# The tenth pair of feature tiles by seven products, with the squares of x summed beside the pairs

## The chip, the cores and the metric

The kernel runs on one core of a Trainium2 chip. The metric is the device time of one execution in microseconds (us). The core has TensorE (PE in the profile, with its weight loads as PEld), VectorE (DVE), ScalarE (ACT), GpSimd (POOL) and SyncE (SP); SP and POOL issue nearly all transfers (DMAs).

## The reference

A trunk of two layers over 512 tokens of width 1024. Layer 0 has latent attention, layer 1 has chunked attention over a shared key and value band; both then have the feed-forward part that the change is in, with a norm ahead of it and one behind it:

```python
def rms_norm(x, g):
    xf = x.astype(jnp.float32)
    y = xf * lax.rsqrt(jnp.mean(xf * xf, axis=-1, keepdims=True) + EPS)
    return (y * g.astype(jnp.float32)).astype(x.dtype)

def swiglu(h, w_gate, w_up, w_down):
    return (jax.nn.silu(h @ w_gate) * (h @ w_up)) @ w_down

for layer in range(DEPTH):
    ...
    x = x + rms_norm(y, attn_post_g[layer])
    h = rms_norm(x, ffn_pre_g[layer])
    f = swiglu(h, ffn_w_gate[layer], ffn_w_up[layer], ffn_w_down[layer])
    x = x + rms_norm(f, ffn_post_g[layer])
```

The feed-forward width is 2816, which is 22 tiles of 128 features.

## The kernel before

Every product of two matrices is computed as three matmuls: each operand is split into a high part (a cast, on ScalarE) and a low part (the remainder, subtracted on VectorE), and high by high, high by low and low by high are added up. `split` (L143 to L145) does this for a chunk of weights of 128 x 1024. The high parts and the low parts of weights have three buffers each, taken in turn, so the fourth chunk's cast waits until the first has been read.

`ffn` runs for each layer. It begins with the output projection of the attention (`out_proj`), in two halves of 256 tokens. Behind each half `Post.apply` norms the result and adds the residual x (L672, L674), which `fetch` has loaded (L683), and splits the new x, times the gain of the next norm, into `xh` and `xl` (L148, L149). The norm's row factor is left out there and comes in later, as a row `rb` that is multiplied into the gate's result.

The 22 tiles of gate and up weights are then treated in three ways:

- tiles 0 and 1 by halves of the tokens, `half(h)`, so that the first can start before the second half of x is there;
- tiles 2 and 3 by whole products, 512 tokens wide, `proj(2, KT, 4, ...)` (L377 to L379): 4 outputs (gate and up of two tiles) x 8 blocks of depth x 3 = 96 matmuls;
- the other 18 tiles as nine pairs in `products`: a product of two-by-two blocks by seven products instead of eight (the scheme of Strassen and Winograd, here on token halves, depth halves and the two tiles of a pair). Each of the seven products, numbered j = 0 to 6, is 24 matmuls of 256 columns (L1550); it needs one chunk of weights (a quarter of the weights or a sum of quarters) and one block or sum of blocks of x.

The outputs of the seven products go to banks of the accumulator memory named be (j = 0 and 6), al (j = 1, 3, 4, 5) and ga (j = 2). `gate` and `up_` (gt and ut) gather them: copies by ScalarE (L1554, L1556, L1560, L1564) and additions by VectorE (L1558, L1562, L1566). Behind j = 6 the pair is finished: gt is multiplied by rb (L1567), ScalarE takes its silu, VectorE multiplies by ut into a hidden tile hd (L1570), and `Hidden` makes sums of hidden tiles (hs, L1271 to L1274) for the down projection, which uses the same seven products.

The sums of weights for a pair: two are formed by DMAs that accumulate into a loaded tile, issued by POOL (L171), two by VectorE (L184). For the first pair, whose `begin` nothing calls, VectorE forms all of them. The sums of x (the `th` and `tl` tiles, made in steps by `blocks_of`) stand beside the whole products.

The squares of the new x are made by ScalarE and added up by VectorE in `sx.squares` (L459, L463) half by half. `total` transposes the sum on TensorE (`tot`, L473) and reduces it; `rstd` takes the power on POOL (L483); `spread_sb` puts the row across partitions by four transposes on TensorE (`bc`, L501) and a copy. Both sets of transposes stand among the whole products. The new x is stored to `mid` in memory ahead of the whole products; the layer's last norm loads it again.

In which order each engine runs its instructions is set when the program is built: a scheduler places them by priorities (`first`, `some`, `weave`, the place in the code) and by explicit orders (`issue_after`); each engine then runs its list in order and waits where an operand or a buffer isn't ready.

Of the kernel before, what the change touches and what calls it, by code (L numbers as in the profile page):

```python
# [19 lines left out]
KT = D // P  # L20
# [7 lines left out]
N_WHOLE = 4  # L28
# [40 lines left out]
def trunk(ctx: ExitStack, tc: tile.TileContext, a, out):  # L69
# [73 lines left out]
    def split(dst_hi, dst_lo, src):  # L143
        return (nc.scalar.copy(dst_hi, src),  # L144
                V.tensor_tensor(dst_lo, src, dst_hi.bitcast(F32), op=OP.subtract))  # L145

    def split_scaled(dst_hi, dst_lo, src, col):
        return (nc.scalar.activation(dst_hi, src, AF.Copy, scale=col),  # L148
                V.scalar_tensor_tensor(dst_lo, src, col, dst_hi.bitcast(F32), op0=OP.mult, op1=OP.subtract))  # L149

    class Pair:
# [4 lines left out]
        def __init__(self, src):  # L156
            self.src, self.raw, self.then, self.made = src, {}, None, False

        def tile(self, n, pool_=wp, tag="raw", bufs=5):
            t = pool_.tile([P, 1024], F32, tag=tag, name=name_("raw"), bufs=bufs)  # L160
            nc.sync.dma_start(t, self.src[n])
            return t

        def begin(self):

            r, self.made = self.raw, True
            r[0] = r[3] = r[6] = self.tile(2, wide[0], "sum", 2)
            r[4] = self.tile(2, wide[0], "sum2", 2)
            for j, n in ((0, 3), (4, 0)):
                with tc.issue_after(last_pow[0].ins):  # L170
                    nc.gpsimd.dma_start(r[j], self.src[n], accum_op=OP.add)  # L171

        def load(self, j):

            if j == 0:
                if not self.made:
                    self.raw[4] = self.tile(2, wide[0], "sum2", 2)
                self.raw[5] = self.tile(3)
            elif j in (1, 2):
                self.raw[j] = self.tile(j - 1)  # L180

        def sums(self, j):
# [4 lines left out]
            if j == 0 and not self.made:  # L187
                r[0] = r[3] = r[6] = wide[0].tile([P, 1024], F32, tag="sum", name=name_("raw"), bufs=2)
                plus(r[0], r[4], r[5])
            elif j in (3, 6):  # L190
                plus(r[j], r[j], r[j // 3])
            elif j == 4 and not self.made:
                plus(r[4], r[4], r[1])
            elif j == 1 and self.then:
# [69 lines left out]
    class Feed:  # L264


        def __init__(self):
            self.plan, self.raw, self.ready, self.pos, self.room = [], [], [], 0, {}
            self.behind, self.gate, self.low = {}, None, None
# [4 lines left out]
        def add_pairs(self, src):  # L274
# [3 lines left out]
            for p, pair in enumerate(pairs):  # L278
                pair.then = pairs[p + 1] if p + 1 < n else None
                for j in range(7):  # L280
                    self.plan.append((pair, 1024, j, None))
# [7 lines left out]
        def load(self, i):  # L289
            while len(self.raw) <= min(i, len(self.plan) - 1):  # L290
# [5 lines left out]
                if isinstance(src, Pair):  # L296
                    src.load(j)
# [8 lines left out]
        def split(self, i):  # L306
            while len(self.ready) <= min(i, len(self.plan) - 1):
# [32 lines left out]
                for c in range(0, 0 if isinstance(raw, list) else n, w):  # L340
                    m = min(w, n - c)
                    with ExitStack() as st:
                        for b in self.behind.get(j, ()):
                            st.enter_context(tc.issue_after(b.ins))
                        if gain is None or isinstance(src, Pair):
                            self.low = split(pieces[c // w][0][:, :m], pieces[c // w][1][:, :m], raw[:, c:c + m])[1]
# [92 lines left out]
    class Sum:  # L439
# [28 lines left out]
        def total(self, h=None, ahead=0):  # L468
# [3 lines left out]
            for i in q:  # L472
                nc.tensor.transpose(t[:, i * P:(i + 1) * P], self.acc[:, i * P:(i + 1) * P], ident)  # L473
# [22 lines left out]

    def spread(col, first=0):

        b = bank("t", "bc")
        for i in range(col.shape[1]):  # L500
            nc.tensor.transpose(b[:, (first + i) * P:(first + i + 1) * P],  # L501
                                col[:, i:i + 1].to_broadcast([P, P]), ident)
# [109 lines left out]
    class Post:  # L612
# [21 lines left out]
        def add_half(self, h, banks, rest, n1, n2, end=None):  # L634
# [7 lines left out]
            with first(200):  # L642
                r = rstd(v)
                fence = V.tensor_copy(small("f")[:, :v.shape[1]], r),
            for n in range(len(feed.ready), len(feed.ready) + 6):
# [21 lines left out]
        def apply(self, x, h, each, to=None):  # L667
            c = HALF[h]
            for k in range(KT):
                t = self.y[k][:, c]  # L670
                with first(80 * h):
# [5 lines left out]
                    each(k, h)  # L677

    def fetch(src, make=U):
        x = []  # L680
        for k in range(KT):
            t = make(name="x")
            nc.sync.dma_start(t, src[:, k])  # L683
            x.append(t)
        return x

    def out_proj(rhs, n_k, post, have, n_last, late):
# [35 lines left out]
        for h in range(2):  # L723
# [17 lines left out]
            if not h:  # L741
                feed.ahead(2 if late else 3)
        return b
# [39 lines left out]
    def plan_ffn(i):  # L783
        for c in range(4):
            feed.add(a["w_gu0"][i, c], 1024, room="h")
        for f in range(N_WHOLE - 2):
            for c in range(2):
                feed.add(a["w_gu"][i, f, c], 1024)
# [345 lines left out]
    def ffn(i, x_src, osp, firsts, late=()):  # L1134
# [10 lines left out]
        x = fetch(x_src)  # L1145
        post = Post(G_APOST[i], H)
        last = out_proj(osp, KT, post, firsts, 2, late)
# [17 lines left out]
        post.add_half(1, last, rest, 9, 14)  # L1165
        run(rest)
        sx.squares(0)
        post.apply(x, 1, sx.each)
        run(half(1))
        sx.squares(1)  # L1170
        for k in range(KT):
            nc.sync.dma_start(a["mid"][:, k], x[k])
        tb = []
        more = blocks_of(x, G_FPRE[i], H, tb)
        next(more)
# [6 lines left out]
        V.tensor_scalar(eps, v, EPS, None, op0=OP.mult)  # L1182
        some(rest, 7)
        rb = spread_sb(r)
        next(more)
        banks.extend(b)
        hid = Hidden(H)


        for f in range(N_WHOLE):  # L1190
            if f < 3:
                b = banks[2 * f:2 * f + 2]
                if f == 2:
                    run(rest)
            else:
                b = [bank(), bank()]
                run(proj(2, KT, 4, xs, b))
            t = U(name="gt")
            V.tensor_tensor(t, b[0], rb, op=OP.mult)
            nc.scalar.activation(t, t, AF.Silu)  # L1200
            h = hid.room()
            V.scalar_tensor_tensor(h, t, -1.0, b[1], op0=OP.mult, op1=OP.mult)
            hid.add(h)
            if f == 1:
                next(more)
        products(xs, tb, rb, hid, by_tokens(H) if i else None)
# [108 lines left out]
    def blocks_of(x, gain, make, out):  # L1315
# [3 lines left out]
        for k in range(KT // 2):  # L1319
# [538 lines left out]
```

## Time and profile before

| | |
|---|---|
| median of 3 runs | 1106.17 us (1105.13 to 1106.2) |
| the profiled execution | 1105.07 us, of which 1103.3 are its span |
| granted TensorE clock, mean of the span | 0.997 of full speed |
| memory read / written in the span | 148.88 MB / 10.88 MB |
| matmuls | 6893 |

The page's rows on engines give busy time, share of the span and number of instructions. A row of the chain in order of time gives start, length, engine, tile and line; a row of a group gives the line, engine, operation and tiles, then how often, busy us and mean ns of one, and the idle time of the engine just before them with its releaser. A row of the DMA issues gives the queue (SPq, POOLq), the count, the size and the median us from issue to landing. Line numbers in the profile are those of the kernel before.

### The profile page before, as it was taken

The page shows a single profiled execution, that of the slowest core. Times are in us where ns is not written, and L with a number is a line of the kernel's source. Part 1 is how long each engine was busy: PE and PEld are TensorE (multiplying, and loading weights), DVE is VectorE, ACT ScalarE, POOL GpSimd, SP SyncE. Part 2 cuts the span into 40 slices and gives each one's busy share as a digit, 9 for nine tenths or more (in the row PEclk, how much of TensorE's full clock was granted, in tenths as well). Part 3 has the DMA queues.
Part 4 walks back from the last instruction along what each step waited for, and adds up shares of the span by engine and source line. Part 5 has one row for each costly group of instructions (what it writes and reads, how often), then busy time and mean ns, then how long its engine had stood idle before and what let it go on. Part 6 is the DMA issues. An engine that isn't in the chain of part 4 may idle for free.

```text
span 1103.3 us, 19079 instructions
## 1 busy us (share of the span) xinstructions
PE 1092.4 (99%) x6893; PEld 978.8 (89%) x6893; DVE 908.5 (82%) x1659; ACT 678.3 (61%) x1323; POOL 117.1 (11%) x181
## 2 busy tenths in 40 slices
PE   9999999999999999999999999999999999999997
PEld 6887889999999998888888888889899999998885
DVE  7787747988878889978858898758988889789977
ACT  7575737655555556668636767657645555556675
POOL 2211100101000001500000110000100010001401
PEclk9999999999999999999999999999999999999999
DMA  7344226447787757961555677634638888758913
GB/s 240 120 116 142 62 68 238 143 116 184 171 202 184 180 167 248 164 191 49 190 153 156 173 192 186 168 121 161 198 103 214 228 207 223 216 178 249 171 29 76
DMA packets 88334, 181.47 MB, mean 164 GB/s; under 512 B 26816, under 2 KB 28608, under 8 KB 88240
## 3 DMA queue, kind: packets, MB, share of 16 engines
q1 hardware_dynamic: 74752, 147.10, 43.1%
q0 software_dynamic: 13056, 32.73, 16.4%
q8 instruction: 54, 0.88, 0.3%
q10 hardware_dynamic: 432, 0.44, 0.1%
q14 instruction: 40, 0.33, 0.1%
HBM read 148.88 MB, written 10.88 MB: 145 GB/s over the span
## 4 chain that ended last, share of the span: by engine, by line
PE 97%; DVE 1%; ACT 1%; issue 1%; DMA 0%; POOL 0%; DVEq 0%; POOLq 0%; SPq 0%; ACTq 0%
PE al L1550 19%; PE b L377 11%; PE b L378 11%; PE b L379 11%; PE be L1550 9%; PE al L1306 8%; PE be L1306 5%; PE ga L1550 5%; PE de L1306 3%; PE ga L1306 3%; PE pt L561 2%; PE b L1707 2%; PE b L1107 1%; PE sc L1699 1%; PE sc L1698 1%
## 5 line engine op out<-in xcount | busy, mean ns | idle before, releaser
L144 ACT CAST whi<-raw 128x1024 fp32r<-128x1024 f32 (+3 forms) x220 | 221.0, 1006 | 205.6 <-PE al L1550 71.5
L145 DVE TENSOR_TENSOR wlo<-raw,whi 128x1024 fp32r<-128x1024 f32 (+3 forms) x220 | 255.8, 1164 | 67.1 <-ACT whi L144 66.1
L1550 PE MATMUL al<-th,whi 128*128 128x256 f32 x432 | 122.8, 284 | 0.0
L1550 PE MATMUL al<-th,wlo 128*128 128x256 f32 x432 | 121.0, 280 | 0.0
L1550 PE MATMUL al<-tl,whi 128*128 128x256 f32 x432 | 121.0, 280 | 0.0
L377 PE MATMUL b<-xh,whi 128*128 128x512 f32 x234 | 96.7, 415 | 0.0
L378 PE MATMUL b<-xl,whi 128*128 128x512 f32 x234 | 91.8, 392 | 0.0
L379 PE MATMUL b<-xh,wlo 128*128 128x512 f32 x234 | 91.7, 392 | 0.0
L1550 PEld LDWEIGHTS al<-th,whi 128*128 128x128 f32 x432 | 81.3, 188 | 2.2
L1550 PEld LDWEIGHTS al<-th,wlo 128*128 128x128 f32 x432 | 81.3, 188 | 0.2 <-DVE wlo L145 0.2
L1550 PEld LDWEIGHTS al<-tl,whi 128*128 128x128 f32 x432 | 81.3, 188 | 0.0
L548 ACT ACTIVATE p<-p,mn 128x128 f32<-128x128 f32 (+1 forms) x96 | 54.1, 563 | 36.0 <-DVE mn L546 34.1
L145 DVE TENSOR_TENSOR ptl<-pt,pth 128x128 fp32r<-128x128 f32 (+1 forms) x96 | 46.6, 485 | 30.5 <-ACT pth L144 29.6
L145 DVE TENSOR_TENSOR wlo<-wd,whi 128x512 fp32r<-128x512 f32 x86 | 56.3, 684 | 14.6 <-ACT whi L144 14.4
L144 ACT CAST whi<-wd 128x512 fp32r<-128x512 f32 x86 | 49.8, 618 | 25.0 <-PE al L1306 10.7
L144 ACT CAST pth<-pt 128x128 fp32r<-128x128 f32 (+1 forms) x96 | 40.3, 422 | 32.2 <-PE pt L561 31.3
L171 POOL DMA_DIRECT2D raw<-in_w_pair x32 | 28.1, 895 | 285.9 <-DVE ut L1562 84.1
L379 PEld LDWEIGHTS b<-xh,wlo 128*128 128x128 f32 x234 | 43.9, 188 | 9.9 <-DVE wlo L145 0.3
L1306 PE MATMUL al<-whi,pl 128*128 128x512 f32 x132 | 51.5, 390 | 0.0
L1306 PE MATMUL al<-wlo,ph 128*128 128x512 f32 x132 | 51.4, 389 | 0.0
L1306 PE MATMUL al<-whi,ph 128*128 128x512 f32 x132 | 51.4, 389 | 0.0
L377 PEld LDWEIGHTS b<-xh,whi 128*128 128x128 f32 x234 | 44.2, 189 | 5.7 <-ACT whi L144 0.2
(320 smaller groups left out, 3391.2 us busy)
## 6 DMA issues: line engine op xcount, KB each, us to landing
raw<-in_w_pair SPq DMA_DIRECT2D x88, 512.0 KB, 4.6
raw<-in_w_pair POOLq DMA_DIRECT2D x32, 512.0 KB, 7.6
wd<-in_w_down SPq DMA_DIRECT2D x54, 256.0 KB, 6.0
raw<-in_w_o SPq DMA_DIRECT2D x16, 512.0 KB, 4.0
raw<-in_w_gu SPq DMA_DIRECT2D x16, 512.0 KB, 4.7
raw<-in_w_down SPq DMA_DIRECT2D x16, 512.0 KB, 4.3
raw<-in_w_qkb SPq DMA_DIRECT2D x16, 512.0 KB, 3.5
wd<-in_w_down POOLq DMA_DIRECT2D x22, 256.0 KB, 5.0
```

The source lines that it names most:

```text
L144: return (nc.scalar.copy(dst_hi, src), V.tensor_tensor(dst_lo, src, dst_hi.bitcast(F32), op=OP.subtract))
L145: V.tensor_tensor(dst_lo, src, dst_hi.bitcast(F32), op=OP.subtract))
L171: nc.gpsimd.dma_start(r[j], self.src[n], accum_op=OP.add)
L377: nc.tensor.matmul(o, l[0], r[0], start=start, stop=False)
L378: nc.tensor.matmul(o, l[0], r[1], start=False, stop=False)
L379: last_mm[0] = nc.tensor.matmul(o, l[1], r[0], start=False, stop=stop)
L548: nc.scalar.activation(p[:, :n], p[:, :n], AF.Exp, bias=mn[:, :1], scale=-1.0, accum_out=self.sums[:, qt:qt + 1])
L561: nc.tensor.transpose(t[:, kt * P:(kt + 1) * P], p[:, kt * P:(kt + 1) * P], ident)
L1107: nc.tensor.matmul(o[:, q_], va[kt][:, part, v_], pt[:, kt, q_], start=n + kt == 0, stop=n == 2 and kt == NQT - 1)
L1306: nc.tensor.matmul(to[e], l[c], r[d], start=j < 4 and k == 0 and n == 0, stop=k == NF // 2 - 1 and n == 2, skip_group_check=True)
L1550: nc.tensor.matmul(o, l[c], r[d], start=first_ and n == 0, stop=k == K2 - 1 and n == 2, skip_group_check=True)
L1707: nc.tensor.matmul(o[:, q_], vv, pt[:, kt, q_], start=pt is pth and kt == 0, stop=pt is ptl and kt == NQT - 1)
```

## The change

`N_WHOLE` goes from 4 to 2: tiles 2 and 3 are no longer computed by whole products but join the pairs, of which there are now ten, and the array of weights for the whole products goes. What stood beside the whole products is placed elsewhere:

- The first pair takes its products in the order 1, 2, 0, 3, 6, 4, 5. All its sums of weights are formed by accumulating DMAs, one into the next (`begin`, `chain`), begun in the half stage.
- x's fetch is ordered behind a load of weights further on (`get_x`), and its token sums are made in more steps, some in the half stage, some beside the first pair.
- x's squares are made beside the first pair: eight by ScalarE, four additions by VectorE, and three accumulating DMAs on POOL's queue (`squares`, `add_squares`). `norm` totals them in the second pair, with an explicit order: product 4 of the second pair stands behind the `tot` transposes, and the third pair's first product behind the `bc` transposes. The results of tiles 0 and 1 are copied out of the accumulator banks (`kept`, fu) until the row is there.
- Finishing a pair (times rb, silu, times ut, the hidden sums) is put into a list of `units`. One is let out at product 6 of the second pair, and from the third pair on one at each of products 1, 3 and 5.
- x is stored to `mid` in the third pair, a block at each product.
- In layer 1 the side work of `by_tokens` (loads, transposes and stores of x for the last norm) starts behind the fifth pair, eight steps a pair, instead of behind the first with four.

```diff
-N_WHOLE = 4
+N_WHOLE = 2
...
+    FIRST_TURN = (1, 2, 0, 3, 6, 4, 5)
...
+        def add(self, j, src, after=None):
+            with behind(after or last_pow[0]):
+                return nc.gpsimd.dma_start(self.raw[j], src, accum_op=OP.add)
+
+        def chain(self):
+
+            self.add(3, self.raw[0])
+            self.add(4, self.src[0], self.add(6, self.raw[3]))
...
             if not h:
                 feed.ahead(2 if late else 3)
+                feed.loaded = get_x(feed.loads[feed.pos + (4 if late else 5)])
...
-        for k in range(KT):
-            nc.sync.dma_start(a["mid"][:, k], x[k])
...
-        b = [bank(), bank()]
-        rest = proj(2, KT, 4, xs, b)
-        some(rest, 3)
-        v = sx.sum.total()
-        r = rstd(v)
...
+        def squares(ks):
+            for k in ks:
+                sq.append(H(name="sq"))
+                nc.scalar.activation(sq[k], x[k], AF.Square, scale=D ** -0.5)
+
+        def add_squares():
+            n = KT // 2
+            for k in range(n):
+                V.tensor_tensor(sq[k], sq[k], sq[k + n], op=OP.add)
+            for n in (2, 1):
+                for k in range(n):
+                    last_pow[0] = nc.gpsimd.dma_start(sq[k], sq[k + n], accum_op=OP.add)
...
+        def norm():
+            sx.sum.acc = sq[0]
+            v = sx.sum.total(None, 300)
+            at[1, 4] = sx.sum.last
...
+        def spread_():
+            rb[0] = spread_sb(rb[0])
+            at[2, 0] = last_bc[0]
...
+        side = {(0, 2): step, (0, 3): step_, (0, 5): add_squares, (1, 3): norm, (1, 6): spread_}
+        side.update(((2, j), lambda j=j: store(j)) for j in range(7))
+        side[3, 0] = lambda: store(7)
+        units = [lambda f=f: gate(*kept[2 * f:2 * f + 2]) for f in range(N_WHOLE)]
+        products(xs, tb, rb, hid, side, units, empty, at, by_tokens(H) if i else None)
...
-            for j in range(7):
-                if aside is not None and p and j in (0, 1, 3, 5):
+            for j in (range(7) if p else FIRST_TURN):
+                if (p, j) in side:
+                    side[p, j]()
+                if p and j in ((6,) if p == 1 else (1, 3, 5)) and units:
+                    units.pop(0)()
+                for _ in range(1 + (j == 3) if aside is not None and p > 4 else 0):
                     next(aside, None)
                 w = feed.next(1024, 2)
+                done = at.get((p, j)) if p else mm
...
                     else:
                         V.tensor_tensor(t[:, A1], t[:, A1], o, op=OP.add)
-                        V.tensor_tensor(t, t, rb, op=OP.mult)
-                        nc.scalar.activation(t, t, AF.Silu)
-                        h = hid.room()
-                        V.tensor_tensor(h, t, u, op=OP.mult)
-                        hid.add(h)
+                        units.append(lambda t=t, u=u: gated(t, u))
+                        while p > 6 and units:
+                            units.pop(0)()
```

Two places in the order of the built program. First TensorE in the second pair (p = 1) of layer 0 of the change. The numbers behind names are buffer numbers; whi and wlo are the high and low parts of a chunk of weights, 2964 and 2965 those of product 3, 3074 and 3075 those of product 6.

```order
L1635 MATMUL al_2969<-tl_2492,whi_2964 128x256
L1635 MATMUL al_2969<-th_2491,wlo_2965 128x256
L1635 MATMUL be_2925<-xh_2286,whi_3074 128x256
L1635 MATMUL be_2925<-xl_2287,whi_3074 128x256
L1635 MATMUL be_2926<-xh_2286,whi_3074 128x256
L1635 MATMUL be_2926<-xl_2287,whi_3074 128x256
L1635 MATMUL be_2925<-xh_2286,wlo_3075 128x256
L1635 MATMUL be_2925<-xh_2292,whi_3074 128x256
```

The last two matmuls of product 3 are followed by product 6, first the four that need only its high part. Sixteen rows on, the same list goes over to the transposes of the squares' sum and to product 4 (weights 2998 and 2999):

```order
L1635 MATMUL be_2926<-xh_2292,wlo_3075 128x256
L1635 MATMUL be_2926<-xh_2298,whi_3074 128x256
L489 MATMUL tot_3030<-ident,sq_2712 128x128 x4
L1635 MATMUL al_2968<-th_2481,whi_2998 128x256
```

So 19 of the 24 matmuls of product 6 stand ahead of `tot` and of products 4 and 5; the other five stand behind the `bc` transposes, at the end of the pair. In the program of before the pairs' products stand in their numbers' order; here the end of a second pair and the first matmuls of a third:

```order
L1550 MATMUL be_2859<-xh_2293,whi_3007 128x256
L1550 MATMUL be_2859<-xl_2294,whi_3007 128x256
L1550 MATMUL be_2859<-xh_2293,wlo_3008 128x256
L1550 MATMUL be_3119<-th_2606,whi_3037 128x256
L1550 MATMUL be_3119<-tl_2607,whi_3037 128x256
```

Second, VectorE at the beginning of the third pair (p = 2) of layer 0. Before, the finishing of the second pair stands among the third pair's subtractions:

```order
L145 TENSOR_TENSOR wlo_3074<-raw_2939,whi_3073 128x1024
L1566 TENSOR_TENSOR gt_2860<-gt_2860,be_2858 128x256
L1567 TENSOR_TENSOR gt_2860<-gt_2860,bc_2714 128x512
L1566 TENSOR_TENSOR gt_2861<-gt_2861,be_2859 128x256
L1567 TENSOR_TENSOR gt_2861<-gt_2861,bc_2714 128x512
L145 TENSOR_TENSOR wlo_3126<-raw_2974,whi_3125 128x1024
L1570 TENSOR_TENSOR hd_3092<-gt_2860,ut_2862 128x512
L1570 TENSOR_TENSOR hd_3109<-gt_2861,ut_2863 128x512
```

In the change the units of tiles 0 and 1 (fu) and of the first pair (gt_2666) stand there:

```order
L146 TENSOR_TENSOR wlo_3152<-raw_2996,whi_3151 128x1024
L1241 TENSOR_TENSOR fu_2639<-fu_2639,bc_3139 128x512
L1656 TENSOR_TENSOR gt_2928<-gt_2928,be_2926 128x256
L146 TENSOR_TENSOR wlo_3189<-raw_3041,whi_3188 128x1024
L1241 TENSOR_TENSOR fu_2641<-fu_2641,bc_3139 128x512
L1244 SCALAR_TENSOR_TENSOR hd_3143<-fu_2639,fu_2640 128x512
L1598 TENSOR_TENSOR gt_2666<-gt_2666,bc_3139 128x512
L146 TENSOR_TENSOR wlo_3235<-raw_2889,whi_3234 128x1024
L1244 SCALAR_TENSOR_TENSOR hd_3221<-fu_2641,fu_2642 128x512
```

From wlo_3152 to the addition that product 5 of the third pair waits for (ut_3185, L1652) the list has 24 instructions in the change: seven 1024 wide, eight 512 wide, nine 256 wide; before, the same stretch (wlo_3074 to ut_3123, L1562) has 20: seven 1024 wide, four 512 wide and nine 256 wide.

More of the change, by code (lines that the diff above doesn't have):

```diff
@@ L676, in apply, with fetch, out_proj @@
                         (nc.gpsimd if k in (0, 2, 4) else V).tensor_tensor(to(k), x[k][:, c], t, op=self.op)
[L677 to L687 removed]
+                    at = each(k, h)
+            return at
+    def fetch(src, x, after=None):
+        with behind(after):
+            for k in range(KT):
+                t = U(name="x")
+                ins = nc.sync.dma_start(t, src[:, k])
+                x.append(t)
+        return ins
+    def out_proj(rhs, n_k, post, have, n_last, late, get_x):
         done = list(have)
@@ L1177, in ffn @@
-        rest = proj(2, KT, 4, xs, b)
-        some(rest, 3)
-        v = sx.sum.total()
-        r = rstd(v)
-        eps = sp.tile([P, 4], F32, tag="eps", name=f"eps_{i}", bufs=1)
[L1182 to L1199, printed above, removed]
+        base = feed.pos
@@ new lines, in ffn @@
+        pair = feed.plan[base][0]
+        pair.chain()
+        feed.behind[base + 2] = feed.behind[base + 3] = post.apply(x, 1, sx.each)
+        next(more)
+        feed.ahead(3)
+        run(half(1))
+        kept = [H(name="fu") for _ in banks]
+        for t, b in zip(kept[:2], banks[:2]):
+            nc.scalar.copy(t, b)
+        with behind(next(more)[0]):
+            for t, b in zip(kept[2:], banks[2:]):
+                empty = nc.scalar.copy(t, b)
+        eps = sp.tile([P, 4], F32, tag="eps", name=f"eps_{i}", bufs=1)
```

172 lines of the change are left out of this document (108 added, 64 removed).

## The prediction

> **What bounds the kernel now.** I read the page's busy times first, then its chain of work that ended last, then that chain in order of time around the place that changes, then a table of stretches, and last the timelines of VectorE and ScalarE inside one pair.
>
> ```profile
> PE 1092.4 (99%) x6893; PEld 978.8 (89%) x6893; DVE 908.5 (82%) x1659; ACT 678.3 (61%) x1323; POOL 117.1 (11%) x181
> PE 97%; DVE 1%; ACT 1%; issue 1%; DMA 0%; POOL 0%; DVEq 0%; POOLq 0%; SPq 0%; ACTq 0%
> ```
>
> TensorE is busy for 99% of the span, and 97% of the chain is its own work. A matmul taken away is therefore worth its own time, and a wait put in front of TensorE costs its own length: there is no slack in which it could vanish. VectorE, at 82%, is the engine with the least to spare behind it.
>
> ```profile
> 212.23 0.23 PE b L377
> ...
> 214.30 0.44 PE tot L473 x4
> ...
> 219.55 0.44 PE bc L501 x4
> ...
> 234.75 0.23 PE b L379
> 234.98 2.82 PE be L1550 x24
> 237.80 2.82 PE al L1550 x24
> 240.61 2.81 PE ga L1550 x24
> ```
>
> This is the chain in layer 0: start, length, what ran. The 96 whole products of feature tiles 2 and 3 run from 212.23 to 234.98 us, with the four transposes of the squares (0.44) and the four that spread the row norm (0.44) among them; then the first pair starts, 24 matmuls in 2.82 us for each of its seven products. TensorE never pauses.
>
> ```profile
> 212.23:234.98 22.75, 22.75 (x106) 18.80 (x106) 20.60 (x42) 13.89 (x24) 2.90 (x3) 1.00 0.39 92
> 787.36:810.08 22.72, 22.72 (x107) 18.80 (x106) 20.09 (x43) 13.78 (x24) 3.22 (x3) 1.00 0.31 70
> 234.98:254.89 19.91, 19.91 (x170) 19.78 (x170) 16.56 (x24) 10.93 (x18) 0.86 (x1) 1.00 0.58 159
> 810.08:830.00 19.92, 19.92 (x170) 19.76 (x169) 17.68 (x25) 11.01 (x17) 0.83 (x1) 1.00 0.50 152
> ```
>
> The columns are the stretch, its length, and the busy time of PE, PEld, DVE, ACT and POOL, then the granted clock, the DMA share and GB/s. Rows one and two are the whole products of the two layers, rows three and four the first pair of each. The clock is 1.00 in all. VectorE is filled to 20.60 of 22.75 us in the stretch that goes, and to 16.56 of 19.91 in a pair.
>
> **The change part by part.**
>
> *The products.* In each layer 96 matmuls of 512 columns go and one pair of 168 matmuls of 256 columns comes. The eight transposes remain. Layer 0: 22.75 - 0.88 = 21.87 us go, 19.91 come: 1.96 us less. Layer 1: 22.72 - 0.88 - 19.92 = 1.92 less. Together **-3.88 us**. By the count of columns alone one eighth of 21.87, 2.73 us a layer, would go; the difference is what the smaller matmuls cost (19.91 / 168 = 0.1185 us for 256 columns, 21.87 / 96 = 0.2278 for 512, so 0.1139 for 256). The Trainium skill says, in Perfetto Trace Analysis, section Optimizing Tensor Performance, that larger matmuls are more efficient than smaller ones; this trace agrees, by 4%, and that is already in the sum above.
>
> *The place of pair 1's last product.* The order excerpt shows that TensorE now runs 19 matmuls of product 6 of pair 1 (weights whi_3074, wlo_3075) straight behind product 3, ahead of the transposes of the squares' sum and of products 4 and 5. There are three buffers for the high parts of weights, so product 6 takes the buffer of product 3, and its cast can start only when product 3 has read it. In the profile of before a pair's seven casts go through the same buffers, but for the order on TensorE; here are some of the second pair's:
>
> ```profile
> 263.26 1.05 ACT L144 CAST whi<-raw 128x1024 fp32r<-128x1024 f32 x1 [1.45 <-PE ga L1550]
> 266.12 1.05 ACT L144 CAST whi<-raw 128x1024 fp32r<-128x1024 f32 x1 [0.96 <-PE al L1550]
> 267.20 1.22 DVE L145 TENSOR_TENSOR wlo<-raw,whi 128x1024 fp32r<-128x1024 f32 x1 [1.63 <-ACT whi L144]
> 269.08 1.05 ACT L144 CAST whi<-raw 128x1024 fp32r<-128x1024 f32 x1 [1.65 <-PE al L1550]
> ```
>
> These are ScalarE's casts and one of VectorE's subtractions (start, length, what, and the idle time before it with what ended that). That pair starts at 254.89, so its product 3 ends four times 2.82 later, at 266.17: the cast of 266.12 is product 6's, released by product 3, done at 267.17; the low part follows from 267.20 to 268.42. So product 6's weights are there 1.0 us (high) and 2.25 us (low) after product 3's end. Before the change, products 4 and 5 (5.64 us) lay over this. Now TensorE stands there: it can do four matmuls that need only the high part (0.47 us), and waits for the rest: 2.25 - 0.47 = **1.8 us**. Behind these matmuls in TensorE's queue stand the transposes and products 4 and 5, whose weights are ready but which can't pass. The transposes also wait for VectorE's addition behind product 6's first half, covered by the five matmuls of the second half (0.59 us against one 256-wide addition): 0 to 0.2.
>
> *Units that were finished in the whole part or in their own pair and now come late.* The gate, silu and Strassen sums of tiles 0 and 1 and of pairs 0 and 1 can't run until the row norm is spread, which now happens behind pair 1. They are let out from the end of pair 1 on, and the order excerpt of VectorE shows them among pair 2's weight subtractions. From wlo_3152 (freed by product 5 of pair 1) to the addition that product 5 of pair 2 waits for, VectorE has 24 instructions: seven of 1024 columns, eight of 512, nine of 256. Their spacing, from a busy stretch of before:
>
> ```profile
> 259.01 1.22 DVE L145 TENSOR_TENSOR wlo<-raw,whi 128x1024 fp32r<-128x1024 f32 x1
> 260.14 0.42 DVE L1272 SCALAR_TENSOR_TENSOR hs<-hs,hd 128x256 f32<-128x256 f32 x1
> 260.48 0.42 DVE L1273 TENSOR_TENSOR hs<-hd,hd 128x256 f32<-128x256 f32 x1
> 260.81 0.42 DVE L1274 SCALAR_TENSOR_TENSOR hs<-hs,hd 128x256 f32<-128x256 f32 x1
> 261.15 1.22 DVE L184 TENSOR_TENSOR raw<-raw,raw 128x1024 f32<-128x1024 f32 x1
> 262.28 1.22 DVE L145 TENSOR_TENSOR wlo<-raw,whi 128x1024 fp32r<-128x1024 f32 x1
> ...
> 274.57 0.69 DVE L1567 TENSOR_TENSOR gt<-gt,bc 128x512 f32<-128x512 f32 x1
> 275.18 0.41 DVE L1566 TENSOR_TENSOR gt<-gt,be 128x256 f32<-128x256 f32 x1
> ```
>
> Start to start: 1.14 (259.01 to 260.14, 261.15 to 262.28), 0.335 and 0.61. So 7 x 1.14 + 8 x 0.60 + 9 x 0.335 = 15.8 us, starting one cast and a hand-over (1.05 + 0.2) behind the end of pair 1's product 5: done 17.05 us behind it. TensorE gets there after the transposes (0.44), five matmuls left of product 6 (0.59), five products (14.1) and three matmuls (0.35): 15.5 us. It waits **1.6 us**. This term is the difference of two long sums: if VectorE is 5% quicker it is 0.8, if one of its instructions waits for ScalarE's table load or silu it is 2.5. Bounds 0 to 2.5. Pair 3 has a unit more than it makes, too, and I add 0.2.
>
> *Pair 0.* Its sums of weights are now a chain of accumulating DMAs, begun in the half stage, so VectorE is spared two 1024-wide additions; in exchange VectorE gets the token sums that it had beside the whole products. By the row of 212.23 VectorE carried 20.60 us there against a pair's 19.91, less the gate work that has moved out; I put its stalls at 0.1 (bounds 0 and 0.7, the surplus).
>
> *x's squares.* Half of the sum is four 512-wide additions (2.4 us) near the end of pair 0, the rest two steps of accumulating DMAs.
>
> ```profile
> raw<-in_w_pair SPq DMA_DIRECT2D x88, 512.0 KB, 4.6
> raw<-in_w_pair POOLq DMA_DIRECT2D x32, 512.0 KB, 7.6
> wd<-raw POOLq DMA_DIRECT2D x22, 256.0 KB, 4.1
> ```
>
> Columns: queue, count, size, median us from issue to landing. The additions stand behind product 4 of pair 0 (sixth in its turn), so they end near 212.2 + 6 x 2.82 + 2.7 = 231.8. With 4.1 us a step (the nearest row: same size, from on-chip memory) the sum lands at 240, with 7.6 (the longest median) at 247. TensorE reaches the transposes at 232.0 + 11.28 + 1.8 + 2.2 = 247.3. So it costs 0 by either; beyond 7.6 each microsecond of a step costs two. The Trainium skill warns, in SBUF — State Buffer, section SBUF: two separate sides, that a DMA issued by GpSimd can starve while VectorE runs a copy in its two-port mode, because its descriptors can't be written. Here the 512 KB rows of the two queues stand 3.0 us apart, accumulation and any such wait together; VectorE's work beside it is additions, and if the rule bit on these too, the steps would be longer than 7.6 and rival four below is the outcome.
>
> *x's fetch* moves behind three loads of weights on SP's queue.
>
> ```profile
> 162.87 4.65 SPq L683 DMA_DIRECT2D x<-in_x  x8
> 168.20 10.15 SPq L303 DMA_DIRECT2D raw<-in_w_gu  x6
> L674 DVE TENSOR_TENSOR x<-x,y x16: 412/418/424, 183.9 to 205.5; 128x256 f32<-128x256 f32 x16
> x<-in_x SPq DMA_DIRECT2D x16, 256.0 KB, 4.7
> ```
>
> Six such loads are issued within 10.15 us from 168.20, so the fifth near 177; x's first goes behind it and lands near 177.3 + 4.7 = 182, 1.9 us before its first use at 183.9. Cost 0, with 1.9 us of cover. The store of mid moves into pair 2, where nothing waits for it.
>
> **Sum.** Per layer 1.8 + 1.6 + 0.1 + 0.2 = 3.7 us of new waits against 1.94 of matmuls saved; both layers have the same order: 7.4 - 3.9 = +3.5. The profiled execution took 1105.07, a span of 1103.3 and 1.8 around it; it is the low end of the runs shown (1105.13 to 1106.2, median 1106.17). 1105.07 + 3.5 = 1108.6; on the median it would be 1109.7. I take the middle, **1109.2**.
>
> **The rivals.**
> 1. *Forecast: both waits appear.* 1109.2. For it: TensorE's order is fixed when the kernel is built, and the rows at 266.12 and 267.20 give the first wait directly. 50%.
> 2. *VectorE keeps up in pair 2.* Only pair 1's wait and 0.3 remain: 2 x 2.1 - 3.9 = +0.3, so 1105.9 on the same footing. It decides if the 24 instructions take 14.2 us instead of 15.8, or the casts come sooner. For it: VectorE idled 1.63 us ahead of the split at 267.20, so it isn't saturated in a pair of before. 22%.
> 3. *The other side, faster: no new wait of any size.* -3.9: 1101.7. It needs product 6's weights ready at product 3's end, that is another free buffer; three casts in flight at 263.26, 266.12 and 269.08, each released by TensorE, speak against it. 12%. That the whole products don't go at all is excluded by the order.
> 4. *A DMA is late besides:* the squares' sum (steps of over 7.6 us) or x (over 1.9 us). With 1 us lost at each place and layer: 1109.2 + 4 = 1113.2. Against it: the rows above; for it: POOL's queue also carries the weight sums of pairs 1 and 2 in these 15 us. 16%.
>
> **How the numbers follow.** About 0.2%, 2.2 us, is what a measurement of this kernel can tell from no change. Slower: rival 4 and the forecast but for its lower edge, 0.63. Same: rival 2 and that edge, 0.25. Faster: 0.12, rival 3. The range leaves out rival 3 and the upper half of rival 4, and takes in the bounds of the two waits (0 and 2.5 in pair 2): 1103.2 to 1113.2.
>
> **What would show it.** Right: in pair 1 TensorE idle for some 1 us, released by ScalarE's cast, and 0.8 us, released by VectorE's subtraction, 11.3 us behind the pair's start; in pair 2 idle for some 1.6 us 14 us behind its start, released by VectorE; pairs 0 and 4 to 9 at 19.9. Wrong: a pair 1 of 19.9 + 0.9 us without idle time, or transposes of the squares that wait for a DMA, or an idle TensorE in the half stage at the first x.

## The result and the profile after

| | us |
|---|---|
| before, median of 4 runs | 1105.65 (1104.34 to 1106.2) |
| changed, median of 4 runs | 1115.9 (1115.18 to 1119.81) |
| ratio | 1.0102, 95% interval 1.0076 to 1.0128 |
| the changed kernel's profiled execution | 1115.27, of which 1113.5 are its span |

The change costs 10.2 us, almost one per cent. The prediction had the sign (1109.2, slower 0.63), not the size: its range ended at 1113.2. One execution of an experiment below, the side work at six steps a pair, ran at a mean granted clock of 0.65 and took 1529.21 us; it is left out of the times.

The page of the changed kernel begins with busy time, share of the span and instructions of each engine:

```profile
span 1113.5 us, 19407 instructions
PE 1090.9 (98%) x7037; PEld 981.6 (88%) x7037; DVE 910.7 (82%) x1657; ACT 692.1 (62%) x1355; POOL 132.2 (12%) x199
```

TensorE's busy time fell by 1.5 us while the span grew by 10.2: what came is waiting. (A pair with a number, as pair 0 or pairs 4 to 7, is counted from 0, as p in the code; the first pair is pair 0.) A table of stretches shows where. The rows are, for each layer, from the first matmul of tiles 2 and 3 to the start of the down projection (length, then busy time of PE, PEld, DVE, ACT and POOL, granted clock, DMA share, GB/s). The kernel before:

```profile
212.23:414.49 202.26, 202.26 (x1616) 197.14 (x1616) 170.49 (x252) 113.27 (x180) 15.18 (x17) 1.00 0.66 170
787.36:989.79 202.43, 202.43 (x1617) 197.34 (x1616) 175.54 (x262) 113.38 (x180) 15.25 (x17) 1.00 0.70 188
```

The changed kernel:

```profile
211.23:415.68 204.45, 201.54 (x1690) 199.60 (x1689) 172.66 (x255) 118.06 (x193) 19.44 (x22) 1.00 0.74 193
787.63:996.38 208.75, 202.95 (x1690) 199.97 (x1689) 177.39 (x263) 117.51 (x193) 19.20 (x22) 1.00 0.81 209
```

Layer 0 is 2.2 us longer, close to the 1.74 that the forecast's terms give (3.7 of waits less 1.96). Layer 1, to which it gave nearly the same, is 6.3 longer. And the span behind these rows, the down projection and the end, went from 1103.3 - 989.79 = 113.5 to 1113.5 - 996.38 = 117.1 us, 3.6 more. So the surprise stands in layer 1: about 4.5 us in its pairs and 3.6 behind them.

Two stretches got shorter and hide a part of it: the one ahead of layer 0's row by 1.0 us, the one between the layers by 0.9. The second gain stands in layer 1's half stage, from its first `tot` transposes to the first matmul of the rows above (before, then changed):

```profile
754.92:787.36 32.44, 32.20 (x267) 31.79 (x266) 29.93 (x76) 21.10 (x49) 1.52 (x2) 1.00 0.52 174
756.10:787.63 31.53, 31.53 (x266) 31.53 (x265) 28.99 (x74) 23.46 (x53) 5.16 (x6) 1.00 0.87 261
```

No term of the forecast speaks of it, and no experiment looks for its cause. Of the 1.0 us ahead of layer 0's row, most stands ahead of its half stage: there the profile of the kernel before is at half the granted clock from 107.5 to 110.9 us, that of the changed kernel at 1.00.

TensorE's waits tell what came. Layer 0 of the changed kernel, from 205 to 420 us (engine and line that waited, for what, us in total, times, longest):

```profile
PE al L1635 <- ACT gt L1642: 1.3, 1, 1.3
PE be L1635 <- ACT whi L144: 1.1, 1, 1.1
PE be L1635 <- DVE wlo L146: 0.5, 1, 0.5
```

The last two are the second pair's product 6 behind product 3, as forecast. The first is in the third pair, but at product 3 and for ScalarE's copy, not at product 5 and for VectorE. Layer 1 of the changed kernel, from 780 to 1020 us:

```profile
PE al L1366 <- ACT ph L144: 2.5, 2, 1.5
PE al L1635 <- DVE wlo L146: 1.6, 2, 1.1
PE al L1635 <- ACT gt L1642: 1.3, 1, 1.3
PE be L1635 <- ACT whi L144: 1.1, 1, 1.1
PE al L1635 <- ACT gt L1647: 1.0, 1, 1.0
PE be L1635 <- DVE wlo L146: 0.5, 1, 0.5
PE al L1366 <- DVE pl L146: 0.5, 1, 0.5
PE al L1635 <- ACT whi L144: 0.3, 1, 0.3
```

The three waits of layer 0 are here again; the other five have no counterpart there (L1366 is the down projection). The one part of the change that layer 0 hasn't is the side work of `by_tokens`: eight steps a pair from the sixth pair on, where before it had four from the second on. VectorE at the start of the ninth pair shows one of its transposes (L1282) and a finished pair's sums (hs) in its list ahead of the weights' sum and split:

```profile
952.13 0.42 DVE L1656 TENSOR_TENSOR gt<-gt,be 128x256 f32<-128x256 f32 x1 [1.43 <-PE be L1635]
952.47 0.42 DVE L1332 SCALAR_TENSOR_TENSOR hs<-hs,hd 128x256 f32<-128x256 f32 x1
952.80 0.42 DVE L1333 TENSOR_TENSOR hs<-hd,hd 128x256 f32<-128x256 f32 x1
953.14 0.42 DVE L1334 SCALAR_TENSOR_TENSOR hs<-hs,hd 128x256 f32<-128x256 f32 x1
953.47 0.68 DVE L1598 TENSOR_TENSOR gt<-gt,bc 128x512 f32<-128x512 f32 x1
954.07 0.70 DVE L1282 STREAM_TRANSPOSE xt<-x 128x512 f32<-128x512 f32 x1
...
955.73 1.22 DVE L202 TENSOR_TENSOR raw<-raw,raw 128x1024 f32<-128x1024 f32 x1
956.86 1.22 DVE L146 TENSOR_TENSOR wlo<-raw,whi 128x1024 fp32r<-128x1024 f32 x1
```

The split that starts at 956.86 ends at 958.1; TensorE stood from 957.1 to 958.1.

### The profile page after: what moved, and what is told of

It reads as the page before. It is cut to its first block, busy times and chain, and to the rows that moved or that the text cites. A ratio compares the mean times of both kernels' runs of the same rounds, so it can differ in the third digit from the quotient of the medians.

```text
span 1113.5 us, 19407 instructions
## 1 busy us (share of the span) xinstructions
PE 1090.9 (98%) x7037; PEld 981.6 (88%) x7037; DVE 910.7 (82%) x1657; ACT 692.1 (62%) x1355; POOL 132.2 (12%) x199
## 5 line engine op out<-in xcount | busy, mean ns | idle before, releaser
L1635 PE MATMUL al<-th,whi 128*128 128x256 f32 x464 | 132.5, 285 | 3.7 <-ACT gt L1642 2.7
L1635 PE MATMUL al<-tl,whi 128*128 128x256 f32 x464 | 130.0, 280 | 0.0
L1635 PE MATMUL al<-th,wlo 128*128 128x256 f32 x464 | 130.0, 280 | 0.0
L1635 PEld LDWEIGHTS al<-tl,whi 128*128 128x128 f32 x464 | 87.4, 188 | 0.0
L393 PE MATMUL b<-xh,whi 128*128 128x512 f32 x170 | 71.7, 422 | 0.0
L185 POOL DMA_DIRECT2D raw<-in_w_pair x40 | 36.1, 931 | 288.0 <-DMA raw<-in_w_pair 68.5
L395 PE MATMUL b<-xh,wlo 128*128 128x512 f32 x170 | 67.1, 395 | 0.2 <-DVE wlo L146 0.2
L394 PE MATMUL b<-xl,whi 128*128 128x512 f32 x170 | 66.8, 393 | 0.0
L1366 PE MATMUL al<-whi,ph 128*128 128x512 f32 x132 | 51.6, 391 | 2.5 <-ACT ph L144 2.5
L1366 PE MATMUL al<-whi,pl 128*128 128x512 f32 x132 | 51.2, 390 | 0.5 <-DVE pl L146 0.5
L1366 PE MATMUL al<-wlo,ph 128*128 128x512 f32 x132 | 51.4, 390 | 0.0
L1635 PE MATMUL be<-xh,whi 128*128 128x256 f32 x160 | 44.8, 281 | 2.1 <-ACT whi L144 2.1
L1635 PE MATMUL al<-xh,wlo 128*128 128x256 f32 x160 | 44.7, 281 | 1.6 <-DVE wlo L146 1.6
```

What stands on the lines that cost most here:

```text
L185: return nc.gpsimd.dma_start(self.raw[j], src, accum_op=OP.add)
L393: nc.tensor.matmul(o, l[0], r[0], start=start, stop=False)
L394: nc.tensor.matmul(o, l[0], r[1], start=False, stop=False)
L395: last_mm[0] = nc.tensor.matmul(o, l[1], r[0], start=False, stop=stop)
L1366: nc.tensor.matmul(to[e], l[c], r[d], start=j < 4 and k == 0 and n == 0, stop=k == NF // 2 - 1 and n == 2, skip_group_check=True)
L1635: mm = nc.tensor.matmul(o, l[c], r[d], start=first_ and n == 0, stop=k == K2 - 1 and n == 2, skip_group_check=True)
```

## The experiments

Each starts from the changed kernel, but for one that starts from the kernel before. Each ratio is to the kernel before on the same chip. Its median was 1105.07 us for the side work over more pairs, the kernel without the transposes, the banks and the copies; 1105.39 for the interval of the six steps a pair; 1104.37 for the others. The changed kernel's 1115.9 stands beside 1105.65. So a difference to the changed kernel compares two chips and is good to about 1 us.

### Layer 1: the side work

*Over more pairs.*

```diff
-                for _ in range(1 + (j == 3) if aside is not None and p > 4 else 0):
+                if aside is not None and p > 3 and j in (0, 1, 3, 5):
                     next(aside, None)
```

> The changed kernel with the side work of layer 1 (loads, transposes and stores of x for the last norm) let out over pairs 4 to 9 with four steps a pair instead of over pairs 5 to 9 with eight. Theory A (the extra 4.6 us of layer 1's pairs and the 3.6 us at the start of its down projection come from side work that is crowded into three pairs, where VectorE and SyncE's queue carry the late units too): the waits of 1.2 us in pair 5 and about 2 us at the start of pairs 8 and 9 and at the down projection shrink by half or more, the execution is 3 to 8 us shorter, 1107 to 1112. Rival B (those waits come from the late units alone, as they stand on VectorE and ScalarE): within 1 us of the changed kernel. Layer 0 has no side work and must not move (204.5 us from the first pair to the down projection).

1116.77 us, no shorter. Its profile has two halves. Layer 1's pairs came down to 205.40, but at the down projection there is more waiting than in the changed kernel:

```profile
790.03:995.43 205.40, 202.17 (x1691) 200.12 (x1689) 173.65 (x255) 118.16 (x193) 19.20 (x22) 1.00 0.78 205
```

```profile
PE al L1366 <- ACT ph L144: 3.1, 2, 2.0
PE al L1366 <- DVE pl L146: 0.8, 1, 0.8
```

With four steps a pair the 24 steps end only with the last pair, and the last two transposes run at 994.9 and 1004.7, the second of them beside the down projection. This fits theory A with the meeting point moved by the edit; by itself it doesn't show it.

*Without the transposes* (the stores take x as it is loaded):

```diff
-            t = make(name="xt")
-            V.transpose(t, x)
+            t = x
```

> The changed kernel without the eight transposes of x on VectorE in layer 1 (the stores take the untransposed x, so the last residual is left out of place); the loads and stores stay. If VectorE's 8 x 0.71 = 5.7 us of transposes and their waits for loads are what delays layer 1: 4 to 8 us shorter than the changed kernel, and the down projection starts without a wait. If the crowded transfers on SyncE's queue delay the weights instead: less than 2 us shorter, and the waits at the down projection stay.

1109.94 us (1107.57 to 1111.49), ratio 1.0033 (1.0015 to 1.0051), 6 us under the changed kernel, and layer 1 is nearly as layer 0; from 780 to 1020 us only this is left:

```profile
PE al L1634 <- ACT gt L1641: 1.3, 1, 1.3
PE be L1634 <- ACT whi L144: 1.1, 1, 1.1
PE be L1634 <- DVE wlo L146: 0.5, 1, 0.5
PE al L1634 <- ACT gt L1646: 0.2, 1, 0.2
```

The loads and stores stayed, so they alone don't make the waits. What goes is VectorE's 5.7 us of transposes, its waits for their loads, and the stores' wait for the transposes, together.

*Earlier: six steps a pair over the fifth to the eighth pair (p = 4 to 7).*

```diff
-                for _ in range(1 + (j == 3) if aside is not None and p > 4 else 0):
+                for _ in range(1 if aside is not None and p > 3 and j < 6 else 0):
                     next(aside, None)
```

> The changed kernel with layer 1's side work let out six steps a pair over pairs 4 to 7, so that it ends three pairs ahead of the down projection; all else as changed, its 24 steps and eight transposes included. Theory A (what costs is where the transposes and late units meet on VectorE's list, at the end of the pairs and the start of the down projection): layer 1's pairs fall from 208.75 to about 205, the waits at the down projection (1.7, 0.6 and 1.2 us) go, 6 to 8 us shorter in all, 1108 to 1110. Theory B (the transposes and transfers cost their sum wherever they stand): less than 2 us shorter.

> The changed kernel with the side work six steps a pair over pairs 4 to 7 once more, for an interval: its profile showed layer 1's pairs at 205.2 us and no wait at the down projection. If the side work's place is worth what that profile shows: 4 to 6 us under the changed kernel's 1115.9, so 1110 to 1112, a ratio of 1.005 to 1.007 to the kernel before. If that profile was a lucky one: 1114 or more.

The first execution gave 1111.02, the repeat a median of 1109.64 (1109.02 to 1110.23), ratio to the kernel before 1.0039 (1.0024 to 1.0053). All eight transposes are there, from 870.8 to 948.9 us instead of 895.5 to 964.0, and in the repeat's profile layer 1 from 780 to 1020 us has the waits of layer 0 and no other (the first one's has 0.6 us more, for ScalarE's copies):

```profile
PE al L1635 <- ACT gt L1642: 1.3, 1, 1.3
PE be L1635 <- ACT whi L144: 1.1, 1, 1.1
PE be L1635 <- DVE wlo L146: 0.5, 1, 0.5
```

So the side work costs about 6 us by where and how densely it stands (1115.9 - 1109.64 = 6.3; 6.0 between the distances to the kernel before), and next to nothing by its amount. Place and density weren't separated: the edit changes both.

*That part alone, put into the kernel before.*

```diff
-                if aside is not None and p and j in (0, 1, 3, 5):
+                for _ in range(1 + (j == 3) if aside is not None and p > 3 else 0):
                     next(aside, None)
```

> The kernel before with one part of the change alone: its side work in layer 1 let out as the change does it, eight steps a pair over the last five pairs instead of four a pair from the second on; nothing else. If crowding alone is the cause of layer 1's extra: 2 to 8 us slower than the kernel before, with waits at the last pairs and the down projection. If it needs the late units as well: within 1.5 us of the kernel before.

1112.1 us (1109.42 to 1114.57), ratio 1.0071 (1.0049 to 1.0093): 7.7 us from this part alone, without late units. The profile is of the longest of the three executions. Its largest wait is in the seventh of the nine pairs, 3.3 us for ScalarE's copies; at the down projection, where waits were expected too, there is none. ScalarE, then SyncE's queue, around the wait:

```profile
939.89 1.04 ACT L144 CAST whi<-raw 128x1024 fp32r<-128x1024 f32 x1 [1.72 <-PE ga L1550]
942.83 0.65 ACT L1556 COPY gt<-al 128x256 f32<-128x256 f32 x2 [1.90 <-DVE hd L1570]
```

```profile
926.54 0.85 SPq L161 DMA_DIRECT2D raw<-in_w_pair  x2
933.84 1.96 SPq L1225 DMA_DIRECT2D out_x<-xt  x4
935.85 0.72 SPq L1219 DMA_DIRECT2D x<-mid  x1
```

The copies, which free the bank that TensorE wants, were let go by a product of the finishing of the pair before (hd), which VectorE began at 942.11. SyncE issued nothing from 927.4 to 933.84, when the stores of a transpose that ran at 933.1 could start; the next loads of weights stand behind them. How much of the 7.7 us is VectorE's list and how much this queue wasn't separated. These aren't the waits of the changed kernel, so the run shows that crowding can cost this much alone, not that it did so there in the same way.

### The second pair: the place of product 6

The program shows why product 6 stands ahead of the transposes. `tot` takes a bank of tag t, of which there are two, and the second pair's be results hold both until product 6 has been added. So with product 4 ordered behind `tot`, product 6 has to come first. The edit gives that pair the two banks of tag s, swaps those of the later pairs, and puts `tot` behind product 3:

```diff
-            be = [bank("t" if p % 2 else "s", "be") for _ in range(2)]
+            be = [bank("t" if p and p % 2 == 0 else "s", "be") for _ in range(2)]
...
+                at["mm"] = mm
                 if (p, j) in side:
...
-        side = {..., (1, 3): norm, (1, 6): spread_}
+        side = {..., (1, 4): norm, (1, 6): spread_}
...
-            v = sx.sum.total(None, 300)
+            with behind(at["mm"]):
+                v = sx.sum.total(None, 300)
```

> The changed kernel with the second pair's be results in the other two accumulator banks (s instead of t, pairs after it swapped too), so that the transposes of the squares' sum find a free bank, and with these transposes placed behind product 3. If the shared banks forced product 6 ahead of the transposes: the second pair's order is 0 to 5, 6, its waits of 1.2 and 0.7 us go in both layers, 3.6 to 4 us shorter in all, 1111 to 1112, and the transposes wait at most 0.3 us, since the squares' sum landed at 240.9 against product 3's end at 242.2. If the squares' sum is what TensorE waits for: the wait stays near 1 us, at the transposes. The swap of banks also re-places ScalarE's instructions in the third pair, copies ahead of the cast, so its wait of 1.5 us may go as well; then 1108 to 1109.

1111.55 us (1110.14 to 1112.42), ratio 1.0057 (1.0032 to 1.0083), 4.3 us under the changed kernel. In layer 0, from 205 to 420 us, one wait is left:

```profile
PE al L1637 <- DVE ut L1654: 0.5, 1, 0.5
```

Both waits of the second pair are gone and `tot` doesn't wait. The third pair's wait for ScalarE went with them, as the expectation had allowed; in its place is the wait for VectorE's addition to ut that the forecast had there. In layer 1 that wait is 1.1 us.

### The third pair: which engine holds TensorE

ScalarE of the changed kernel in that pair (start, length, what, and the idle time before with what ended it):

```profile
260.16 1.04 ACT L144 CAST whi<-raw 128x1024 fp32r<-128x1024 f32 x1
262.55 1.04 ACT L144 CAST whi<-raw 128x1024 fp32r<-128x1024 f32 x1 [1.35 <-issue]
263.50 0.64 ACT L1642 COPY gt<-al 128x256 f32<-128x256 f32 x2
```

The cast at 262.55 is product 5's; it needs product 2's buffer, so it starts when product 2 ends. The two copies behind it in the list have had their data since product 1, and product 3 needs the banks they empty. Idle ScalarE, idle TensorE, and the cause is the order of two instructions. The edit orders that cast behind the copies:

```diff
-                            nc.scalar.copy(t[:, A0], o)
+                            got = nc.scalar.copy(t[:, A0], o)
+                        if p == 2:
+                            feed.behind[feed.pos + 3] = [got]
```

> The changed kernel with one explicit order more: in the third pair ScalarE's cast of product 5's weights stands behind the copies of product 1's results, not ahead of them. If the wait of 1.5 us at product 3 of that pair (seen behind these copies in both layers) comes from ScalarE's order: it goes, 1.3 to 1.5 us in each layer, 2 to 3 us in all, 1112 to 1113.5. If VectorE's queue of late units sets it, as forecast: the wait moves two products on, to product 5, keeps 1.0 to 1.6 us, and the time stays within 1 us.

1114.13 us (1113.19 to 1117.08), ratio 1.0087 (1.0054 to 1.0121), 1.8 under the changed kernel: between the two theories, and not clear of the spread of either kernel's runs. The profile, of the longest of the three, shows what the time can't. Layer 0, from 205 to 420 us:

```profile
PE be L1635 <- ACT whi L144: 1.1, 1, 1.1
PE al L1635 <- DVE ut L1654: 0.6, 1, 0.6
PE be L1635 <- DVE wlo L146: 0.5, 1, 0.5
```

ScalarE's wait has gone, and VectorE's appears two products on. TensorE's spacing has 1.50 us too much at the one place in the changed kernel and 0.72 at the other here. ScalarE's wait had covered VectorE's; the two don't add up. Layer 1 has the same two waits of 1.1 and 0.5 us and VectorE's of 0.6.

### The edits together

The three edits (side work over pairs 4 to 7, banks, copies):

> Three edits together: the second pair's be banks with the transposes behind product 3, ScalarE's copies ahead of the cast in the third pair, and the side work six steps a pair over pairs 4 to 7. If the three causes add up: the waits of 1.2 and 0.7 us (second pair), 1.5 us (third pair) and those of layer 1 are gone in both layers, what stays is VectorE's wait of 0.7 to 1.3 us at product 5 of the third pair; 1104 to 1106, about the kernel before. If the edits only move one wait to the next: 1108 or more.

1103.35 us (1101.9 to 1106.99, 8 runs), ratio to the kernel before 0.9998 (0.9987 to 1.0009): no difference, from 10.2 us slower. The largest wait left is VectorE's in layer 1's third pair:

```profile
PE al L1637 <- DVE ut L1656: 1.2, 1, 1.2
```

With one edit more, which takes three 512-wide instructions out of VectorE's list ahead of that addition:

```diff
-            V.tensor_tensor(t, t, rb[0], op=OP.mult)
+            with behind(at.get("late")):
+                V.tensor_tensor(t, t, rb[0], op=OP.mult)
...
-                        V.tensor_tensor(u[:, A1], o, u[:, A1], op=OP.add)
+                        got = V.tensor_tensor(u[:, A1], o, u[:, A1], op=OP.add)
+                        if p == 2:
+                            at["late"] = got
```

> As the three edits together, and one more: from the unit of the first pair's second tile on, the multiplication by the row norm stands behind the additions of product 4 in the third pair, so that VectorE has three 512-wide instructions fewer (1.8 us) ahead of the addition that product 5 waits for. If the forecast's count of VectorE's instructions is what sets that wait: it goes (0.7 and 1.3 us), and the time falls below the kernel before, 1102 to 1104. If something else holds product 5 (its cast or its load): the wait stays, 1104 to 1106.

1101.29 us (1100.63 to 1102.42, 6 runs), ratio 0.997 (0.9958 to 0.9983): 3.1 us faster than the kernel before. VectorE's wait has gone, so its list set it, and not the cast or the load of product 5. The two layers' stretches are now

```profile
212.05:412.40 200.35, 200.35 (x1691) 199.30 (x1689) 171.93 (x255) 118.18 (x193) 19.43 (x22) 1.00 0.74 197
784.37:986.33 201.96, 201.54 (x1691) 200.24 (x1689) 176.05 (x263) 118.04 (x193) 19.20 (x22) 1.00 0.81 217
```

Against the kernel before layer 0 has gained 202.26 - 200.35 = 1.91 us; the forecast's term for the products alone was 1.96. So in layer 0 the tenth pair is worth what its matmuls say, once nothing waits. Layer 1 has gained only 202.43 - 201.96 = 0.47 of 1.92; 0.4 us of waits for ScalarE's copies are left there, and about 1 us stays unexplained.

## Why the prediction was right and wrong

- **The products, -3.88:** right as far as shown. Layer 0 without waits gained 1.91 of 1.96; layer 1, not quite without them, 0.47 of 1.92.
- **Product 6 in the second pair, 1.8 a layer:** right, in place, size and releasers: 1.06 us behind ScalarE's cast and 0.51 behind VectorE's split by the profile's count, 1.22 and 0.68 by the spacing of the matmuls, in both layers. The prediction took the order as given; its reason, the two banks of tag t, came from the experiment. That the clock can fall behind such waits, as the last section shows, it didn't say.
- **The third pair, 1.6 a layer behind VectorE:** the size was right by luck, the engine wrong. The wait was 1.5 us and ScalarE's. VectorE's own wait at product 5, when uncovered, was by the profile 0.5 us (banks) and 0.6 (copies) in layer 0 and 0.6 to 1.2 in layer 1; with the three edits together layer 0 had none. That is below 1.6, as can befall a difference of two long sums, and within its bounds of 0 to 2.5. The prediction counted the list of one engine and left the other's unread, where a cast stood ahead of two copies.
- **Pair 0, the squares' sum, x's fetch at nothing:** right. The first pair had no wait. The accumulating DMAs of the squares landed in 3.4 us at the median, under the 4.1 of the prediction's nearest row, and the transposes never waited. The starved transfers of which the Trainium skill warns (SBUF — State Buffer, section SBUF: two separate sides) aren't seen beside these additions.

```profile
sq<-sq POOLq DMA_DIRECT2D x6, 256.0 KB, 3.4
```

- **"Both layers have the same order": the step that failed.** It holds for the parts that the prediction priced. The side work of layer 1 is a part of the change, and no term of the sum and no rival spoke of it; where it stood cost about 6 us of the 10.2. Moved earlier, all eight transposes kept, the kernel is at 1109.64, 4.3 over its kernel before, where the sum had 3.5. That this is so close is in part luck: layer 0's row is 2.2 longer and not 1.74, and layer 1's half stage, at which the sum had nothing, is 0.9 shorter. VectorE wasn't fuller with the crowded transposes: from 895 to 975 us it was busy for 16.1 to 17.3 of each 20 us, in the kernel before from 830 to 909.6 for 17.0 to 17.6 of each 19.9. So a count of its work would not have found the cost; its order would, as in the list at 952.13, and a transpose waits for its load in front of everything behind it (1.8 us, once, in the changed kernel).
- **The range:** it took in what the sum could be off by, but nothing for a part that the sum didn't hold.

## What to carry to other kernels

Work that is cheap by its amount can be dear by its place: side work with eight transposes of 0.7 us cost about 6 us crowded into three pairs near a stage's end, and next to nothing when it began a pair earlier and was spread over four. Before a sum is trusted, every part of the change needs a line in it, and every in-order engine's list around the place has to be read for an instruction that waits ahead of one that is ready; the wait that shows may cover a second. Where an order looks odd, look for a shared buffer that forces it.

## What the runs showed of the hardware

In the kernel before with the crowded side work, the wait of 3.3 us has a price of its own. These stretches surround it (the granted clock stands third from the end):

```profile
936.00:940.00 4.00, 3.97 (x34) 3.76 (x33) 3.89 (x4) 1.81 (x3) 0.00 (x0) 1.00 0.98 154
940.00:943.00 3.00, 0.00 (x0) 0.00 (x0) 2.60 (x4) 1.10 (x2) 0.00 (x0) 0.84 1.05 397
943.00:946.00 3.00, 2.75 (x13) 2.75 (x14) 2.99 (x8) 0.48 (x2) 0.86 (x1) 0.50 0.41 81
946.00:950.00 4.00, 4.00 (x24) 4.00 (x24) 0.30 (x1) 1.69 (x3) 0.00 (x0) 0.64 1.05 181
```

TensorE idled from 940.0 to 943.25. If the clock is either 1.00 or 0.50, the means of 0.84 and 0.64 put its fall at about 942.0 and its return at about 948.9, 6.8 us later. Behind the wait the matmuls stood 0.213 us apart in place of 0.118, some 25 of them, so the wait cost 2.4 us more.

It can follow shorter waits too. The copies edit leaves the second pair's waits of 1.1 and 0.5 us as they are, and behind them its profile has, in layer 0 and in layer 1:

```profile
246.50:249.80 3.30, 3.30 (x17) 3.30 (x17) 0.81 (x2) 0.00 (x0) 0.00 (x0) 0.50 1.05 271
823.30:826.70 3.40, 3.40 (x18) 3.40 (x17) 1.21 (x3) 0.00 (x0) 0.00 (x0) 0.50 1.03 259
```

The repeat of the six steps a pair has it in layer 0. In the profile of the changed kernel the same waits left the clock at 1.00. Some 16 matmuls at 0.213 us are, by estimate, 1.5 us more for the same waits in one execution and nothing more in another.

The Trainium skill has this in TensorE: Matmul & The Clock Gate, section Part 1: an idle window of about 3.4 us halves the clock. The half agrees with these rows. That TensorE has to idle for all of 3.4 us doesn't: the clock fell about 2 us into the wait of 3.3 us, and behind waits of 1.1 and 0.5 us.
